# A macaron encoder block: score runs of one half of the heads over four banks, and the last output tile in two halves

## The chip, the cores and the metric

One core of a Trainium2 chip runs the whole block: two feed-forward parts, a recurrence (RG-LRU), neighbourhood attention and the projections between them, all in float32. The metric is the device time in microseconds. A profile of one execution shows each engine: PE is TensorE (matmuls), DVE is VectorE, ACT is ScalarE, SP issues most DMAs.

## The reference, cut to what matters

```python
def _neighbourhood_attention(q, k, v, rpb):          # 16 heads of 64, tokens on an 8 x 64 grid
    ...
    def row_block(args):
        ...
        s = jnp.einsum('bnqhd,brnkhd->bnhqrk', q_r, k_r, preferred_element_type=jnp.float32)
        ...
        s = s + jnp.transpose(bias, (0, 2, 3, 1, 4))[None]
        s = jnp.where(mask, s, -jnp.inf)
        shp = s.shape
        p = jax.nn.softmax(s.reshape(shp[:4] + (kr * K_COLS,)), axis=-1).reshape(shp)
        return jnp.einsum('bhnqrk,brnkhd->bnqhd', p.astype(v.dtype), v_r)
...
        y = jax.nn.sigmoid(ga) * y_lru + jax.nn.sigmoid(gb) * y_att
        x = x + y @ w_out[l]

        x = x + FFN_RES * _swiglu(_rmsnorm(x, norm_ffn2[l]), w_ffn2_gu[l], w_ffn2_down[l])
```

The 512 tokens lie on 8 rows of 64. Queries come in four column blocks of 16 columns; each block sees 32 columns of keys in all 8 rows, so a block has 128 queries and 256 keys.

## The kernel before, in words

Activations stand with 128 features on the partitions and 512 tokens along the row. To hold float32 accuracy each operand is cut into a high and a low part, and a product is three matmuls: high by high, high by low, low by high (`mm3`, L144; lines L145 to L147). Weights are loaded by SP, cut by ACT (L118) and DVE (L121), and used in runs of 24 matmuls of 512 columns per output tile.

The instructions are laid out by a planner: it walks them in the order in which the program emits them, and where an instruction's inputs or its buffer aren't ready by the planner's reckoning, it takes a later one that is ready. Each engine's queue then runs in the order so found. The eight PSUM banks are two pools of four: `acc` (the projections' tiles) and `aux` (transposes, scores, attention's output).

Attention is a generator, `heads(hf, ...)` at L710, for each half `hf` of the heads; a feature tile `fi` (four per half) holds two heads, `hp`. The main stream is projections: for the second half it is the gates (`gates`, L842, one tile of 24 matmuls per call). After each tile `weave` (L449) moves the generator on, by 0.75 steps for a gates tile, so that one step, or none, lies behind each tile. `until` (L462) moves it on by force where a result is needed. The steps of a half:

- `start(fi)` (L727): 4 transposes of q and 4 of k into two `aux` banks (L731, L733), and four copies out of them: qh and kh on ACT (L737, L739), ql and kl on DVE (L738, L740).
- `scores(fi, n2)` (L744): column blocks 2 n2 and 2 n2 + 1. For each block the three products (qh, kh), (qh, kl), (ql, kh), each for both heads; a head is 64 of the 128 rows of the array, and the two heads write two different `aux` banks (L757). That is a run of twelve matmuls. Behind it come, per head and block, the read with bias and maximum on DVE (L767), the exponential on ACT (L770), and the scaling by the sum on DVE (L772, L776). The read frees the bank.
- `turn(fi, n2, hp)` (L780): 4 transposes of p into an `aux` bank (L784), copied out by ACT (L786).
- `apply(fi)` (L789): 32 matmuls of p by v, which use 64 columns of the array each (L795), into an `aux` bank, copied out by ACT (L804).

The loop at L809 to L829 sets the order: eight units (fi, n2); a unit's `turn` comes one unit later and `apply` of a tile two units after its second half, right behind that unit's scores (the order is fixed by `after`, L199). `start(fi + 1)` stands behind the first unit of tile fi.

At the end `ffn` (L334) does the down projection in two groups of four output tiles. For the first 16 of the 22 feature tiles the four outputs advance together (`put_in`, L426); then each output does its last 6 feature tiles alone, is scaled on DVE (L442) and handed to `out2` (L899), which adds the residual (L901) and writes 256 KB (L902).

Of the kernel before, what the change touches and what calls it, by code (L numbers as in the profile page):

```python
# [12 lines left out]
ALU = mybir.AluOpType  # L13
# [3 lines left out]
P = 128  # L17
T = 512
D = 1024
KT = D // P  # L20
# [26 lines left out]

DTAIL = 3

AHEAD = 4  # L50
NWARM = 8

# [1 line left out]

LRU_F = 4

ATT_LAG = 1, 2

RATE = {
    "xr": {"lru": 4, "att": 0.0},  # L60
# [7 lines left out]
def block_kernel(ctx: ExitStack, tc, a, out):  # L68
# [18 lines left out]
    def big_t(dt=F32, shape=(P, T), n="b"):  # L87
        return big.tile(list(shape), dt, tag="big", bufs=NBIG, name=nm(n))
# [4 lines left out]
    def acc_t():  # L93
        return acc.tile([P, T], F32, tag="acc", name=nm("acc"))

    def aux_t():
        return aux.tile([P, T], F32, tag="aux", name=nm("aux"))
# [43 lines left out]
            split(raw[:, s], H[:, s], L[:, s], act)  # L141
        return H, L

    def mm3(ps, wh, wl, xh, xl, first, last):  # L144
        nc.tensor.matmul(ps, wh, xh, start=first, stop=False)  # L145
        nc.tensor.matmul(ps, wh, xl, start=False, stop=False)  # L146
        nc.tensor.matmul(ps, wl, xh, start=False, stop=last)  # L147

    def feat_chunk(src, nk, xh, xl, ps, k0, ktot, act=True):
        H, L = load_w(src, nk * P, act)  # L150
# [183 lines left out]
    def ffn(wgu, ws, wd, xh, xl, S, ssum, plain, res, emit_out, lead=None):  # L334
        hs = []
        r = None
        pre = {}
        if lead is not None:


            for i in range(NLEAD):
                pre[i] = acc_t() if i < 3 else aux_t()
            wts = [[None] * 2 for _ in range(NLEAD)]
            for k in range(KT):
                lead[0](k)
                if k in LEAD_W:
                    n = LEAD_W[k]
                    o = (k % 4) * P
                    s = slice(o, o + n * P)
                    for i in range(NLEAD):  # L350
                        if k % 4 == 0:
                            wts[i][k // 4] = big_t(n="wraw"), big_t(F32R, n="wh"), big_t(F32R, n="wl")
                        q = nc.scalar if k == 0 and i % 2 == 0 else nc.sync
                        tc.keep_in_program_order(
                            q.dma_start(wts[i][k // 4][0][:, s], wgu[i][:, k * P : (k + n) * P]))
                if k == 0:
                    for raw, H, L in [wts[i][0] for i in range(NLEAD)]:
                        cast = nc.vector.tensor_copy(H[:, s], raw[:, s])
                    after(lead[1](k), cast)
                    for raw, H, L in [wts[i][0] for i in range(NLEAD)]:  # L360
                        nc.vector.tensor_tensor(L[:, s], raw[:, s], H[:, s].bitcast(F32), ALU.subtract)
                else:
                    lead[1](k)
                    if k in LEAD_W:
                        for raw, H, L in [wts[i][k // 4] for i in range(NLEAD)]:
                            split(raw[:, s], H[:, s], L[:, s])
                s = slice((k % 4) * P, (k % 4 + 1) * P)
                w = [wts[i][k // 4] for i in range(NLEAD)]
                lead[2](k)
                if k == KT - 1:  # L370
                    r = rstd(ssum)[0]
                for i in range(NLEAD):
                    nc.tensor.matmul(pre[i], w[i][1][:, s], xh[k], start=k == 0, stop=False)  # L373
                for i in range(NLEAD):
                    nc.tensor.matmul(pre[i], w[i][1][:, s], xl[k], start=False, stop=False)
                for i in range(NLEAD):
                    nc.tensor.matmul(pre[i], w[i][2][:, s], xh[k], start=False, stop=k == KT - 1)

            lead[3]()

        def chunk(i):
            if i in pre:
# [24 lines left out]
        cuts = {}  # L407

        def ahead(n):
            while len(cuts) < min(n, len(order)):  # L410
                qk = order[len(cuts)]
                cuts[qk] = big_t(F32R, n="hh"), big_t(F32R, n="hl")
                split(hs[qk[1]], *cuts[qk])

        strassen(ws, (FT - plain) // 2, A, r, hs, lambda: ahead(AHEAD))
        for q in range(2):
            outs = range(q * 4, q * 4 + 4)
            for i in range(2):
# [7 lines left out]
            def put_in(i, k):  # L426
                H, L = ws_[k // 2]
                c = slice((k % 2) * T + i * P, (k % 2) * T + (i + 1) * P)
                mm3(ps[i], H[:, c], L[:, c], *cuts[q, k], k == 0, k == FT - 1)

            for j in range(FT // 2):
                ws_.append(load_w(wd[q, j], 1024))
                ahead(q * FT + 2 * j + 2 + AHEAD)
                if j < FT // 2 - DTAIL:
                    for k in (2 * j, 2 * j + 1):
                        for i in range(4):
                            put_in(i, k)
            for i, m in enumerate(outs):
                for k in range(FT - 2 * DTAIL, FT):
                    put_in(i, k)  # L440
                t = big_t(n="dn")
                nc.vector.scalar_tensor_tensor(t, ps[i], -0.5, r, ALU.mult, ALU.mult)  # L442
                emit_out(m, t)


    lanes = {"lru": [], "att": []}
# [263 lines left out]
    def heads(hf, raws, st):  # L710
# [30 lines left out]
            grid = lambda t: t.rearrange("p (r c) -> p r c", r=ROWS)  # L741
            qk[fi] = qh, ql, grid(kh), grid(kl)

        def scores(fi, n2):  # L744

            qh, ql, kh, kl = qk[fi]
            if n2 == 0:
                rss[fi] = tiny.tile([P, 2, NCB], F32, tag="rs", name=nm("rs"))
            rs = rss[fi]
            ps = [aux_t() for _ in range(2)]  # L750
            for i in range(2):
                n = n2 * 2 + i
                keys = lambda t: t[:, :, KSTART[n] : KSTART[n] + 2 * QC].rearrange("p r (h c) -> p h r c", h=2)
                for q_, k_ in ((qh, kh), (qh, kl), (ql, kh)):
                    for hp in (1, 0):
                        o = slice(hp * HD, (hp + 1) * HD)
                        mm = nc.tensor.matmul(ps[hp][:, i * 256 : (i + 1) * 256], q_[o, n * P : (n + 1) * P], keys(k_[o]),  # L757
                                         start=k_ is kh and q_ is qh, stop=q_ is ql)
# [53 lines left out]
        LB, LC = ATT_LAG  # L812
        for i in range(len(units) + LC):
            if i < len(units):
                fi, n2 = units[i]
                last = scores(fi, n2)
                if i >= LC and units[i - LC][1]:
                    apply(units[i - LC][0], last)
                if n2 == 0:
# [81 lines left out]
        nc.vector.tensor_tensor(o, ps, xres[m], ALU.add)  # L901
        nc.sync.dma_start(out[m], o)  # L902

    ffn(a["w2gu"], a["w2s"], a["w2d"], xh, xl, forms.S, ssum, NPLAIN[1], lambda m: xd[m], out2)


def layouts(inp):
# [72 lines left out]
```

## Time and profile before

| | |
|---|---|
| median of 3 runs | 1133.14 us (1133.12 to 1133.49) |
| the profiled execution's own time | 1133.02 us |
| its span, first to last instruction | 1130.9 us |
| TensorE busy | 1124.3 us, 99% of the span |
| VectorE busy | 836.0 us, 74% |
| ScalarE busy | 594.7 us, 53% |
| granted TensorE clock, mean | 0.999 of full speed |

The span leaves out what lies around the first and last instruction. Matmuls are pipelined: a printed duration overlaps the next matmul's, so the cost of one is the distance between two starts. The timeline merges neighbouring instructions of one kind into one line.

### The profile page before, as it was taken

The page shows a single profiled execution, that of the slowest core. Times are in us where ns is not written, and L with a number is a line of the kernel's source. Part 1 is how long each engine was busy: PE and PEld are TensorE (multiplying, and loading weights), DVE is VectorE, ACT ScalarE, POOL GpSimd, SP SyncE. Part 2 cuts the span into 40 slices and gives each one's busy share as a digit, 9 for nine tenths or more (in the row PEclk, how much of TensorE's full clock was granted, in tenths as well). Part 3 has the DMA queues.
Part 4 walks back from the last instruction along what each step waited for, and adds up shares of the span by engine and source line. Part 5 has one row for each costly group of instructions (what it writes and reads, how often), then busy time and mean ns, then how long its engine had stood idle before and what let it go on. Part 6 is the DMA issues. An engine that isn't in the chain of part 4 may idle for free.

```text
span 1130.9 us, 17246 instructions
## 1 busy us (share of the span) xinstructions
PE 1124.3 (99%) x6872; PEld 995.1 (88%) x6872; DVE 836.0 (74%) x1288; ACT 594.7 (53%) x896; POOL 19.3 (2%) x52
## 2 busy tenths in 40 slices
PE   9999999999999999999999999999999999999998
PEld 8899999988888888888788888888999999998886
DVE  7898888884836798797855576859688888894542
ACT  8554544563624595985564254656445445464330
POOL 0000000000000000010110000000000000000000
PEclk9999999999999999999999999999999999999999
DMA  7242333443433342353443332355123233352320
GB/s 263 94 131 79 119 102 102 136 137 94 130 94 111 94 159 84 112 167 103 132 149 104 93 103 88 109 169 184 56 93 116 92 112 113 94 168 93 131 75 38
DMA packets 43553, 130.69 MB, mean 116 GB/s; under 512 B 5968, under 2 KB 8272, under 8 KB 43472
## 3 DMA queue, kind: packets, MB, share of 16 engines
q1 hardware_dynamic: 39600, 119.36, 33.8%
q0 software_dynamic: 3296, 9.97, 2.8%
q8 instruction: 54, 0.88, 0.3%
q10 hardware_dynamic: 576, 0.26, 0.1%
q14 instruction: 27, 0.22, 0.1%
HBM read 121.17 MB, written 8.39 MB: 115 GB/s over the span
## 4 chain that ended last, share of the span: by engine, by line
PE 97%; DVE 1%; ACT 1%; issue 0%; DVEq 0%
PE acc L260 29%; PE acc L145 11%; PE acc L146 11%; PE acc L147 11%; PE aux L260 5%; PE aux L145 4%; PE aux L146 4%; PE aux L147 4%; PE acc L666 4%; PE acc L665 3%; PE acc L667 3%; PE aux L784 1%; PE aux L795 1%; PE aux L757 1%; PE acc L373 1%; PE aux L373 0%
## 5 line engine op out<-in xcount | busy, mean ns | idle before, releaser
L118 ACT ACTIVATE wh<-wraw 128x1024 fp32r<-128x1024 f32 (+3 forms) x242 | 241.3, 999 | 333.9 <-PE acc L260 96.8
L121 DVE TENSOR_TENSOR wl<-wraw,wh 128x1024 fp32r<-128x1024 f32 (+3 forms) x254 | 291.4, 1150 | 138.5 <-ACT wh L118 137.9
L260 PE MATMUL acc<-s,wh 128*128 128x256 f32 x1216 | 220.6, 283 | 0.1
L260 PEld LDWEIGHTS acc<-s,wh 128*128 128x128 f32 x1216 | 189.7, 192 | 0.3 <-ACT p L317 0.3
L260 PE MATMUL acc<-s,wl 128*128 128x256 f32 x608 | 172.1, 283 | 0.0
L145 PE MATMUL acc<-xh,wh 128*128 128x512 f32 x304 | 120.2, 395 | 0.0
L146 PE MATMUL acc<-xl,wh 128*128 128x512 f32 x304 | 119.0, 392 | 0.0
L147 PE MATMUL acc<-xh,wl 128*128 128x512 f32 x304 | 118.8, 391 | 0.0
L260 PEld LDWEIGHTS acc<-s,wl 128*128 128x128 f32 x608 | 116.7, 192 | 0.0
L260 PE MATMUL acc<-xh,wl 128*128 128x256 f32 x304 | 86.0, 283 | 0.0
L260 PE MATMUL acc<-xl,wh 128*128 128x256 f32 x304 | 86.0, 283 | 0.0
L260 PE MATMUL acc<-xh,wh 128*128 128x256 f32 x304 | 86.0, 283 | 0.0
L665 PE MATMUL acc<-wh,xh 128*128 128x512 f32 x192 | 75.2, 392 | 0.0
L666 PE MATMUL acc<-wh,xl 128*128 128x512 f32 x192 | 74.8, 390 | 0.0
L667 PE MATMUL acc<-wl,xh 128*128 128x512 f32 x192 | 74.8, 389 | 0.0
L294 DVE TENSOR_TENSOR wraw<-wraw,pair 128x1024 f32<-128x1024 f32 x57 | 69.5, 1220 | 0.8
L145 PE MATMUL aux<-hh,wh 128*128 128x512 f32 x176 | 68.5, 389 | 0.0
L146 PE MATMUL aux<-hl,wh 128*128 128x512 f32 x176 | 68.5, 389 | 0.0
L147 PE MATMUL aux<-hh,wl 128*128 128x512 f32 x176 | 68.5, 389 | 0.0
L145 PE MATMUL acc<-hh,wh 128*128 128x512 f32 x176 | 68.5, 389 | 0.0
L146 PE MATMUL acc<-hl,wh 128*128 128x512 f32 x176 | 68.5, 389 | 0.0
L147 PE MATMUL acc<-hh,wl 128*128 128x512 f32 x176 | 68.5, 389 | 0.0
(194 smaller groups left out, 2197.5 us busy)
## 6 DMA issues: line engine op xcount, KB each, us to landing
wraw<-wqkv SPq DMA_DIRECT2D x24, 512.0 KB, 3.6
wraw<-wg SPq DMA_DIRECT2D x24, 512.0 KB, 3.6
wraw<-w1d SPq DMA_DIRECT2D x22, 512.0 KB, 3.6
wraw<-w2d SPq DMA_DIRECT2D x22, 512.0 KB, 3.6
pair<-w2s SPq DMA_DIRECT2D x20, 512.0 KB, 3.6
wraw<-w2s SPq DMA_DIRECT2D x20, 512.0 KB, 3.6
wraw<-w1s SPq DMA_DIRECT2D x18, 512.0 KB, 3.6
pair<-w1s SPq DMA_DIRECT2D x18, 512.0 KB, 3.6
```

What stands on the lines that cost most here:

```text
L118: nc.scalar.activation(H, raw, AF.Copy)
L121: nc.vector.tensor_tensor(L, raw, H.bitcast(F32), ALU.subtract)
L145: nc.tensor.matmul(ps, wh, xh, start=first, stop=False)
L146: nc.tensor.matmul(ps, wh, xl, start=False, stop=False)
L147: nc.tensor.matmul(ps, wl, xh, start=False, stop=last)
L260: nc.tensor.matmul(o, w_[:, c], x_, start=first and m + k == 0 and w_ is H and x_ is xh_, stop=m + k == 4 and w_ is L, skip_group_check=True)
L294: nc.vector.tensor_tensor(t, t, o, ALU.add)
L373: nc.tensor.matmul(pre[i], w[i][1][:, s], xh[k], start=k == 0, stop=False)
L665: nc.tensor.matmul(pss[j], xh[kk][:, tj], H[:, s], start=kk == 0, stop=False)
L666: nc.tensor.matmul(pss[j], xl[kk][:, tj], H[:, s], start=False, stop=False)
L667: nc.tensor.matmul(pss[j], xh[kk][:, tj], L[:, s], start=False, stop=kk == KT - 1)
L757: mm = nc.tensor.matmul(ps[hp][:, i * 256 : (i + 1) * 256], q_[o, n * P : (n + 1) * P], keys(k_[o]), start=k_ is kh and q_ is qh, stop=q_ ...
```

## The change

In the first half of the heads nothing changes but the order of the three products: k's low part comes first, (qh, kl), (qh, kh), (ql, kh). In the second half a unit is a whole feature tile: its four column blocks are one run of 24 matmuls, the first two blocks into two `aux` banks, the other two into two `acc` banks. The lag of `turn` is one unit and that of `apply` two units, now in units of a tile. A unit has two steps (a `yield` stands between its two halves of `turn`), so the number of steps stays 14.

The last output tile (m = 7) is done in halves of 256 tokens for its last five feature tiles: the first half goes on in the tile's bank, the second half's share goes into a bank of its own, `p2`, and is added on DVE. Each half is written by a DMA of its own.

```diff
+EHALF = 5
...
-ATT_LAG = 1, 2
+ATT_LAG = (1, 2), (1, 2)
...
             for i, m in enumerate(outs):
+                if end is not None and m == KT - 1:
+                    break
                 for k in range(FT - 2 * DTAIL, FT):
                     put_in(i, k)
...
+        i, x, k0 = 3, xres[KT - 1], FT - EHALF
+        for k in range(FT - 2 * DTAIL, k0):
+            put_in(i, k, k0 - 1)
+        t, o, p2 = big_t(n="dn"), big_t(n="o"), aux_t()[:, :half]
+        t0, t1 = slice(0, half), slice(half, T)
+
+        def scaled(p, tok):
+            nc.vector.scalar_tensor_tensor(t[:, tok], p, -0.5, r[:, tok], ALU.mult, ALU.mult)
+
+        for k in range(k0, FT):
+            put_half(ps[i][:, t0], i, k, t0, False, k == FT - 1)
+        for k in range(k0, FT):
+            put_half(p2, i, k, t1, k == k0, k == FT - 1)
+        scaled(ps[i][:, t1], t1)
+        nc.vector.tensor_tensor(o[:, t1], t[:, t1], x[:, t1], ALU.add)
+        scaled(ps[i][:, t0], t0)
+        nc.vector.tensor_tensor(o[:, t0], t[:, t0], x[:, t0], ALU.add)
+        end(t0, o)
+        scaled(p2, t1)
+        nc.vector.tensor_tensor(o[:, t1], o[:, t1], t[:, t1], ALU.add)
+        end(t1, o)
...
-        def scores(fi, n2):
+        def scores(fi, n2s):
...
-            ps = [aux_t() for _ in range(2)]
-            for i in range(2):
-                n = n2 * 2 + i
+            pss = {n2: [aux_t() if n2 == n2s[0] else acc_t() for _ in range(2)] for n2 in n2s}
+            for n in [n2 * 2 + i for n2 in n2s for i in range(2)]:
+                ps, i = pss[n // 2], n % 2
...
-                for q_, k_ in ((qh, kh), (qh, kl), (ql, kh)):
+                for q_, k_ in ((qh, kl), (qh, kh), (ql, kh)):
...
-            for hp in range(2):
+            for n2, hp in [(n2, hp) for n2 in n2s for hp in range(2)]:
+                ps = pss[n2]
...
-        units = [(fi, n2) for fi in range(4) for n2 in range(2)]
+        units = [(fi, (n2,)) for fi in range(4) for n2 in range(2)] if hf == 0 else [(fi, (0, 1)) for fi in range(4)]
...
             if 0 <= i - LB < len(units):
-                for hp in range(2):
-                    turn(*units[i - LB], hp)
-            if len(units) <= i < len(units) + LC and units[i - LC][1]:
+                for n2 in units[i - LB][1]:
+                    for hp in range(2):
+                        turn(units[i - LB][0], n2, hp)
+                    if hf == 1 and n2 == 0:
+                        yield
+            if len(units) <= i < len(units) + LC and 1 in units[i - LC][1]:
                 apply(units[i - LC][0])
             yield
```

The new `put_half` is `put_in` for half the tokens: one feature tile's three matmuls (`mm3`) of 256 columns into a given part of a bank. The new `end` of `ffn` writes one half of the last tile, `out[KT - 1][:, tok]`.

## Rows read from the trace of the kernel before

**Rows 1.** The page, part 1: busy time, share of the span, instructions of each engine.

```profile
PE 1124.3 (99%) x6872; PEld 995.1 (88%) x6872; DVE 836.0 (74%) x1288; ACT 594.7 (53%) x896; POOL 19.3 (2%) x52
```

**Rows 2.** The page, part 4: engines' shares of the chain that ended last.

```profile
PE 97%; DVE 1%; ACT 1%; issue 0%; DVEq 0%
```

**Rows 3.** Timeline, TensorE, first runs, second half: start us, us, engine, line, out<-in.

```profile
655.62 0.39 PE L147 MATMUL acc<-xh,wl 128*128 128x512 f32 x1
...
655.94 0.38 PE L757 MATMUL aux<-kh,qh 64*128 64x256 f32 x2
...
656.16 0.28 PE L757 MATMUL aux<-kl,qh 64*128 64x256 f32 x2
...
656.28 0.28 PE L757 MATMUL aux<-kh,ql 64*128 64x256 f32 x2
...
657.70 0.48 PE L145 MATMUL acc<-xh,wh 128*128 128x512 f32 x1
...
663.35 0.39 PE L757 MATMUL aux<-kh,qh 64*128 64x256 f32 x2
```

**Rows 4.** Timeline, TensorE: ahead of and behind eight transposes without a run.

```profile
643.84 0.40 PE L147 MATMUL acc<-xh,wl 128*128 128x512 f32 x1
...
644.87 0.48 PE L145 MATMUL acc<-xh,wh 128*128 128x512 f32 x1
```

**Rows 5.** Timeline, TensorE: ahead of and behind a run that a product follows.

```profile
684.53 0.39 PE L147 MATMUL acc<-xh,wl 128*128 128x512 f32 x1
...
685.76 0.66 PE L795 MATMUL aux<-PT,v 128*64 128x128 f32 x8
```

**Rows 6.** Timeline, TensorE: a product without a run ahead of it.

```profile
614.52 0.39 PE L147 MATMUL acc<-xh,wl 128*128 128x512 f32 x1
614.84 0.66 PE L795 MATMUL aux<-PT,v 128*64 128x128 f32 x8
...
616.74 0.50 PE L145 MATMUL acc<-xh,wh 128*128 128x512 f32 x1
```

**Rows 7.** Timeline, TensorE: ahead of p's transposes, twice.

```profile
673.30 0.39 PE L145 MATMUL acc<-xh,wh 128*128 128x512 f32 x1
673.81 0.66 PE L784 MATMUL aux<-ident,p 128*128 128x128 f32 x4
...
696.46 0.40 PE L147 MATMUL acc<-xh,wl 128*128 128x512 f32 x1
697.09 0.66 PE L784 MATMUL aux<-ident,p 128*128 128x128 f32 x4 [0.24 <-DVE nmx L767]
```

**Rows 8.** Timeline, ScalarE: first and last exponential behind the run of 655.94.

```profile
659.52 0.51 ACT L770 ACTIVATE p<-so,nmx 128x256 f32<-128x256 f32 x1
...
661.01 0.49 ACT L770 ACTIVATE p<-so,nmx 128x256 f32<-128x256 f32 x1
```

**Rows 9.** Timeline, VectorE: a read of scores, and the copy of kl.

```profile
658.16 0.42 DVE L767 CUSTOM_DVE_ANT_0 so<-aux,bm 128x256 f32<-128x256 f32 x1
...
663.02 0.74 DVE L740 SCALAR_TENSOR_TENSOR kl<-aux,small,kh 128x512 fp32r<-128x512 f32 x1
```

**Rows 10.** Timeline, all engines: the last matmuls and what follows them.

```profile
1125.89 0.39 PE L146 MATMUL acc<-hl,wh 128*128 128x512 f32 x1
...
1126.12 0.39 PE L147 MATMUL acc<-hh,wl 128*128 128x512 f32 x1
1126.55 0.69 DVE L442 SCALAR_TENSOR_TENSOR dn<-acc,rstd 128x512 f32<-128x512 f32 x1 [2.66 <-PE acc L147]
1127.27 0.69 DVE L901 TENSOR_TENSOR o<-dn,pair 128x512 f32<-128x512 f32 x1
```

**Rows 11.** DMA strip, 1127 to 1131 us: 40 slots, busy share in tenths.

```profile
DMA  0000000000000000005999997100000000000000
```

**Rows 12.** Chain in order of time: start us, us, what; 24 matmuls of 256 columns.

```profile
131.93 2.88 PE aux L260 x24
```

**Rows 13.** Groups by form, VectorE: count, busy us, mean ns; 256 columns.

```profile
L211 DVE SCALAR_TENSOR_TENSOR s<-s,xg 128x256 f32<-128x256 f32 x16 | 6.7, 421 | 0.3
```

More of the change, by code (lines that the diff above doesn't have):

```diff
@@ L142, in load_w, with mm3 @@
         return H, L
[L144 to L147, printed above, removed]
+    def mm3(ps, wh, wl, xh, xl, first, last, skip=False):
+        nc.tensor.matmul(ps, wh, xh, start=first, stop=False, skip_group_check=skip)
+        nc.tensor.matmul(ps, wh, xl, start=False, stop=False, skip_group_check=skip)
+        nc.tensor.matmul(ps, wl, xh, start=False, stop=last, skip_group_check=skip)
     def feat_chunk(src, nk, xh, xl, ps, k0, ktot, act=True):
@@ L332, in strassen, with ffn @@
         last_product(prev)
-    def ffn(wgu, ws, wd, xh, xl, S, ssum, plain, res, emit_out, lead=None):
+    def ffn(wgu, ws, wd, xh, xl, S, ssum, plain, res, emit_out, lead=None, end=None):
         hs = []
@@ L424, in ffn, with put_in, put_half @@
             ws_ = []
-            def put_in(i, k):
+            def put_in(i, k, last=FT - 1):
                 H, L = ws_[k // 2]
                 c = slice((k % 2) * T + i * P, (k % 2) * T + (i + 1) * P)
-                mm3(ps[i], H[:, c], L[:, c], *cuts[q, k], k == 0, k == FT - 1)
+                mm3(ps[i], H[:, c], L[:, c], *cuts[q, k], k == 0, k == last)
+            def put_half(o, i, k, tok, first, last):
+                H, L = ws_[k // 2]
+                c = slice((k % 2) * T + i * P, (k % 2) * T + (i + 1) * P)
+                mm3(o, H[:, c], L[:, c], *(t[:, tok] for t in cuts[q, k]), first, last, True)
             for j in range(FT // 2):
@@ L443, in ffn @@
                 emit_out(m, t)
+        if end is None:
+            return
+        i, x, k0 = 3, xres[KT - 1], FT - EHALF
[17 more added lines that the diff above has]
+        end(t1, o)
     lanes = {"lru": [], "att": []}
@@ L742, in start @@
             qk[fi] = qh, ql, grid(kh), grid(kl)
-        def scores(fi, n2):
+        def scores(fi, n2s):
             qh, ql, kh, kl = qk[fi]
-            if n2 == 0:
+            if 0 in n2s:
                 rss[fi] = tiny.tile([P, 2, NCB], F32, tag="rs", name=nm("rs"))
             rs = rss[fi]
-            ps = [aux_t() for _ in range(2)]
-            for i in range(2):
-                n = n2 * 2 + i
+            pss = {n2: [aux_t() if n2 == n2s[0] else acc_t() for _ in range(2)] for n2 in n2s}
+            for n in [n2 * 2 + i for n2 in n2s for i in range(2)]:
+                ps, i = pss[n // 2], n % 2
                 keys = lambda t: t[:, :, KSTART[n] : KSTART[n] + 2 * QC].rearrange("p r (h c) -> p h r c", h=2)
-                for q_, k_ in ((qh, kh), (qh, kl), (ql, kh)):
+                for q_, k_ in ((qh, kl), (qh, kh), (ql, kh)):
                     for hp in (1, 0):
@@ L757, in scores @@
                         mm = nc.tensor.matmul(ps[hp][:, i * 256 : (i + 1) * 256], q_[o, n * P : (n + 1) * P], keys(k_[o]),
-                                         start=k_ is kh and q_ is qh, stop=q_ is ql)
-            for hp in range(2):
+                                         start=k_ is kl, stop=q_ is ql)
+            for n2, hp in [(n2, hp) for n2 in n2s for hp in range(2)]:
+                ps = pss[n2]
                 bm = bms[hf * 4 + fi, hp]
@@ L806, in apply @@
             att[hf * 4 + fi] = at
-        units = [(fi, n2) for fi in range(4) for n2 in range(2)]
+        units = [(fi, (n2,)) for fi in range(4) for n2 in range(2)] if hf == 0 else [(fi, (0, 1)) for fi in range(4)]
         start(0)
         yield
-        LB, LC = ATT_LAG
+        LB, LC = ATT_LAG[hf]
         for i in range(len(units) + LC):
             if i < len(units):
-                fi, n2 = units[i]
-                last = scores(fi, n2)
-                if i >= LC and units[i - LC][1]:
+                fi, n2s = units[i]
+                last = scores(fi, n2s)
+                if i >= LC and 1 in units[i - LC][1]:
                     apply(units[i - LC][0], last)
-                if n2 == 0:
+                if 0 in n2s:
                     if fi < 3:
@@ L902, in out2 @@
         nc.sync.dma_start(out[m], o)
-    ffn(a["w2gu"], a["w2s"], a["w2d"], xh, xl, forms.S, ssum, NPLAIN[1], lambda m: xd[m], out2)
+    ffn(a["w2gu"], a["w2s"], a["w2d"], xh, xl, forms.S, ssum, NPLAIN[1], lambda m: xd[m], out2,
+        end=lambda tok, o: nc.sync.dma_start(out[KT - 1][:, tok], o[:, tok]))
 def layouts(inp):
```

## The prediction

> **What bounds the kernel now.** I read the busy shares first: TensorE is busy 99% of the span, no other engine more than 74% [rows 1]. The chain that ended last says the same from the other side: 97% of it is TensorE [rows 2]. So a change counts here only by what it takes from, or adds to, TensorE's own stream, and by what lies behind the last matmul. Two places are touched: the score runs of the second half of the heads (from 655.9 us on), and the last output tile. I then read TensorE's timeline there by start times, because matmuls are pipelined: the distance from one start to the next is the cost, not the printed duration. A 512-column matmul costs 0.23 us (1125.89 to 1126.12) [rows 10].
>
> **Part 1: fewer score runs.** A run of before is twelve matmuls on 64 of the 128 rows, issued as six pairs that run side by side; within a run a pair costs 0.12 us (656.16 to 656.28) [rows 3], so six cost 0.72. What a whole run costs I take from two stretches that differ by the run alone. With a run ahead of the eight q and k transposes, the last gates matmul starts at 655.62 and the next gates matmul at 657.70: 2.08 us [rows 3]. With the same eight transposes and no run it is 643.84 to 644.87: 1.03 us [rows 4]. The run costs 1.05, so 0.33 us of it is entering and leaving. It can be seen where: 0.32 instead of 0.23 ahead of the first pair, 0.22 instead of 0.12 between the first pair and the second, the rest behind the last pair. A run with the values' product (L795, which uses 64 of the columns) right behind it goes from 684.53 to 685.76, 1.23 us [rows 5]; that product alone is entered in 0.32 (614.52 to 614.84) [rows 6], so this run costs 0.91, of which 0.19 is overhead: the entry to the product is paid with or without it.
> The second half has eight runs: five lead back to full-array work (0.33 each) and three lead into a product (0.19 each), 2.22 us. After the change four runs of twelve pairs are left. By the loop, the first two are followed by transposes and the last two by a product: 2 x 0.33 + 2 x 0.19 = 1.04. All 96 matmuls stay. The third product loses its run ahead of it, but its own entry was in neither sum. So **part 1 takes off 1.18 us**. Bounds: 0.8 if four runs save only the smaller overhead (4 x 0.19), 1.3 if each saves the larger.
> Overhead at both ends of a run is what the rows show. The Trainium skill (TensorEngine Tiling (Array Packing), Key Properties) has a rule for it: changing the tiling mode drains TensorE. By the Trainium skill's other page on it (TensorE: Matmul & The Clock Gate, Step-by-step: what each phase is for) a drain is some 128 cycles, an estimated 0.05 us at 2.4 GHz; eight switches fewer would then give 0.4 us in place of 1.18, and a time of 1132.0. The rows show three times that, so this price gets no chance of its own.
>
> **Part 2: k's low part first.** The same three products in another order: no instruction more, no byte more. What moves is a wait: a run can't start before kl (L740, the last of the four copies of a feature tile) exists, where it used to start on kh and qh. In the first half of the heads, and for tiles 2 and 3 of the second half, two steps of the weave lie between the copies and the run, each with a gates tile of 24 matmuls at least, so I cost it at nothing there. For tile 1 of the second half the cover is gone: its run moves one step forward, to where the run of 663.35 stands now [rows 3], with 24 gates matmuls between the transposes and it. Today ScalarE does four exponentials there (one per 0.50 us: 659.52 to 661.01 is three steps) [rows 8], then the q and k copies, and VectorE ends kl at 663.02 + 0.74 = 663.76 [rows 9]. With eight exponentials in front of the copies kl comes 4 x 0.50 = 2.0 us later, at 665.75. TensorE gets there at 663.35 + 0.72 = 664.07. The gap is 1.7 us. It costs all of that if TensorE's queue holds the run next, and nothing if the planner has put seven matmuls of the next gates tile ahead (7 x 0.23 = 1.6). Queued behind it are that tile's matmuls, so the whole stream waits.
> The trace shows how well such filling works: in front of p's transposes the planner puts in gates matmuls, and what is left over is 673.30 to 673.81, less 0.23, 0.28 us, and 696.46 to 697.09, less 0.23, 0.40 us [rows 7]. These waits are for the score reads (L767) to free banks. I take 0.40 for kl (bounds 0 and 1.7).
>
> **Part 3: banks.** A run now fills four banks, two of them from the pool of the gates. The reads of the first two can begin 0.72 us before the run ends, which helps the transposes that want those banks. The two gates banks are held until the seventh and eighth read. Of four banks, one holds the tile just done, two the run, one is free; the next tile takes that one for 24 x 0.23 = 5.5 us, and eight reads of 0.42 us [rows 9], 3.4 us, are over by then: no wait. The two waits of [rows 7], 0.68 us, become one behind run 1 and one behind run 2, where a product of 1.9 us (614.84 to 616.74) [rows 6] now lies between and covers most: I take 0.28 in all. With the 0.40 for kl, **the waits come out as they went in: 0**, with bounds of -0.7 (both vanish) and +1.7 (the kl gap uncovered).
>
> **Part 4: the last tile by halves.** Before: the last matmul starts at 1126.12, the scaling at 1126.55, the addition at 1127.27, each 0.69 us [rows 10]; then the DMA. TensorE's side: the last five of the 22 feature tiles go from 15 matmuls of 512 columns (15 x 0.23 = 3.45) to 30 of 256. Those cost 0.12 each (24 in 2.88 us) [rows 12], 3.60: plus 0.15. The first half's two DVE steps and the early part of the second (four operations, 1.7 us) lie beside the second half's 15 matmuls (1.8 us). Behind the last matmul one scaling and one addition of 256 columns remain, 0.42 us each [rows 13] in place of 0.69: minus 0.54. The output DMA moved its 256 KB in 0.75 us (the strip has a slot of 0.1 us) [rows 11]; 128 KB at that rate is 0.37: minus 0.37, bounds 0 (rows half as long cost as much) and 0.37. The extra DMA's issue falls a microsecond before the last one. **Part 4 takes off 0.76 us**, bounds 0.4 and 0.8.
>
> **Sum.** -1.18 + 0 - 0.76 = -1.94 us. The profiled execution took 1133.02 us (span 1130.9, 2.1 around it), 0.12 under the median of 1133.14. Set against the median: **1131.2 us**. A difference of 0.2%, 2.3 us, is about what can be told from no change: under 1130.9 or over 1135.4.
>
> **Rivals.**
> *Waits vanish.* The banks of the first half of a run are read earlier, the planner covers kl, and the two waits go: another -0.7 to -1.1, so 1130.2 to 1130.6. For it: a product lies ahead of the transposes in two of the four runs. Against: the 0.28 and 0.40 are left over although gates matmuls fill in [rows 7], and the reads come no faster than now.
> *The reads become the bound; slower.* One run now hands VectorE eight reads and ScalarE eight exponentials at once. The wait that would grow is kl's (1.7), and behind it the transposes of three runs that want banks, each by the four reads more that may stand ahead, 4 x 0.42 = 1.7 us: at most 1.7 + 3 x 1.7 = 6.8, in place of the 0.7 there now. At half of it, 3.4 - 0.7 = +2.7, less 1.9, it gives +0.8: 1133.9. It decides from waits of 2.6 us (0.7 + 1.9) in this half on. Against: the gates matmuls fill, and two of the three have a product as cover. The Trainium skill names this mechanism (TensorEngine Tiling (Array Packing), PSUM Bottleneck: tiling speeds up TensorE but not the emptying of PSUM); in the trace it shows only as the 0.28 and 0.40.
> *It doesn't do what it says.* The second pair of banks isn't free where the run is planned, gates matmuls slip in between, and the eight runs stay: only part 4 is left, 1132.4. For it: the gates' own tile is still to be read. Against: one bank of four is held by it.
>
> **How the numbers follow.** Forecast (1130.9 to 1132.0): 0.55, as it needs only start distances that repeat in all eight runs. Waits vanish: 0.20. Split runs, or a tail that gains nothing: 0.15. Reads become the bound: 0.10, of which 0.03 above 1135.4. Faster than 1130.9: 0.20 and the lower edge of the forecast, 0.23. Slower than 1135.4: 0.03. The same: 0.74. The range runs from 1130.1 (part 1 and 4 at their upper bounds and no waits) to 1133.2 (the kl gap whole and the lower bounds of the rest, and the split runs).
>
> **What would show it.** In the changed profile: four runs of 24 score matmuls in the second half, each 0.12 per pair after the first; 0.32 ahead of a run's first pair; how long TensorE stands ahead of the run of tile 1 near 664 us, and whether kl released it; gates matmuls inside a run (split). At the end: 30 matmuls of 256 columns 0.12 apart, two operations of 0.42 us behind the last of them, and the last DMA's strip half as wide. The forecast is wrong if transposes wait more than a microsecond for L767, if kl's wait is more than 1.7 us, or if other stages, whose code is unchanged, are laid out differently by the planner.

## The result, and the profile after

| | before | after |
|---|---|---|
| median of 8 runs each | 1133.3 us (1133.04 to 1133.73) | 1136.71 us (1135.71 to 1137.25) |
| ratio after / before, 95% interval | | 1.0029 (1.0019 to 1.0038) |
| the profiled execution's own time | 1133.02 us | 1137.16 us |
| its span | 1130.9 us | 1135.4 us |

The change costs 3.4 us where I had forecast a gain of 1.94: slower, beyond the upper end of the range and on the other side of zero. The runs of after fall into two groups, 1135.71 to 1136.33 and 1137.09 to 1137.25, with a mean granted TensorE clock of 0.998 and 0.997; the profiled execution is of the upper one, so its account comes out larger (4.5 us of span) than the medians do.

Part 1 of the page of after (busy us, share, instructions of each engine), beside [rows 1]:

```profile
PE 1125.2 (99%) x6887; PEld 998.0 (88%) x6887; DVE 836.2 (74%) x1292; ACT 594.0 (52%) x896; POOL 19.3 (2%) x52
```

It says almost nothing: TensorE is still busy 99%. What went wrong covers a dozen microseconds of 1135. The waits of TensorE in after (what waited, for whom, us in total, times, longest) are plainer:

```profile
PE aux L791 <- DVE kl L774: 3.7, 1, 3.7
...
PE aux L819 <- ACT att L839: 1.0, 1, 1.0
```

Both are new and lie in the second half of the heads; of the three lines left out two have their like in before, and the third is 0.2 us. L791 is the score matmul (L757 of before), L774 the copy of kl (L740), L819 p's transposes (L784), L839 the copy of attention's output out of its bank (L804).

TensorE's timeline in after around the first of them (start us, us, engine, line, out<-in, and in brackets the idle time and who ended it):

```profile
663.95 0.39 PE L149 MATMUL acc<-xh,wl 128*128 128x512 f32 x1
667.99 0.58 PE L791 MATMUL aux<-kl,qh 64*128 64x256 f32 x2 [3.65 <-DVE kl L774]
668.34 0.45 PE L791 MATMUL aux<-kh,qh 64*128 64x256 f32 x2
668.55 0.45 PE L791 MATMUL aux<-kh,ql 64*128 64x256 f32 x2
...
670.85 1.11 PE L765 MATMUL aux<-ident,qk 128*128 128x128 f32 x4
671.75 1.06 PE L767 MATMUL aux<-ident,qk 128*128 128x128 f32 x4
672.61 1.57 PE L819 MATMUL aux<-ident,p 128*128 128x128 f32 x8
673.94 0.48 PE L147 MATMUL acc<-xh,wh 128*128 128x512 f32 x1
...
696.72 0.40 PE L149 MATMUL acc<-xh,wl 128*128 128x512 f32 x1
698.16 0.66 PE L819 MATMUL aux<-ident,p 128*128 128x128 f32 x4 [1.05 <-ACT att L839]
```

Two things are to be seen. TensorE stands still from 664 to 668. And what comes after that is slow: a pair costs 0.21 us (668.34 to 668.55) where it cost 0.12 in [rows 3], four transposes 0.90 (670.85 to 671.75). The busy time of each engine by stretch in after (stretch, us, then PE, PEld, DVE, ACT, POOL busy with counts, granted TensorE clock, DMA share, GB/s) shows why:

```profile
656.00:664.00 8.00, 8.00 (x57) 6.76 (x56) 7.99 (x30) 6.63 (x18) 0.60 (x2) 1.00 0.30 82
664.00:668.00 4.00, 0.35 (x4) 0.04 (x2) 3.85 (x8) 1.92 (x4) 0.48 (x1) 0.86 0.50 166
668.00:674.00 6.00, 6.00 (x41) 5.78 (x41) 4.32 (x25) 3.86 (x15) 0.54 (x1) 0.53 0.41 112
674.00:680.00 6.00, 6.00 (x31) 5.00 (x30) 2.93 (x8) 2.30 (x6) 0.54 (x1) 1.00 0.35 109
```

The granted clock is 1.00 when TensorE stops, 0.53 over the six microseconds after it starts again (nearly all of it at the lower of the two levels, 1.2 GHz), and 1.00 afterwards. "Busy 6.00" in that stretch is work at half speed; that is why the share of busy time hides it.

By slices of half a microsecond the clock is down before TensorE starts again; this is the first slice that is wholly at the lower level:

```profile
667.00:667.50 0.50, 0.00 (x0) 0.00 (x0) 0.50 (x2) 0.00 (x0) 0.00 (x0) 0.50 0.03 12
```

**The account.** From the first transposes of the second half to the first matmul with w_out: 644.08 to 737.71 in before, 93.63 us; 644.26 to 742.92 in after, 98.66. The difference is +5.03:

| term | us |
|---|---|
| wait for kl: 663.95 to 667.99, 4.04, less the usual entry 0.32 [rows 3] | +3.72 |
| low clock: the run of 24 matmuls 2.86 (the three others 1.65), q and k transposes 1.76 (0.85), p's transposes 1.33 (0.85) | +2.60 |
| wait for the copy of attention's output: 696.72 to 698.16, 1.44, less 0.23 | +1.21 |
| four runs instead of eight (part 1) | -1.18 |
| waits of before that are gone: 0.28 and 0.40 [rows 7]; between 727 and 738 us eight of p's transposes at 1.21 and 0.96 (0.85 and 0.88 are usual there) and a product at 2.10 (1.90 [rows 6]) | -1.32 |
| sum | +5.03 |

The part 1 term is not measured by itself: it is the forecast's own figure, and the sum closes with it. Ahead of this stage after is 0.18 later; behind it, from w_out's first matmul to the end of the span, it is 0.71 faster (393.19 to 392.48), which is part 4. 0.18 + 5.03 - 0.71 = 4.50, the difference of the spans.

**Why kl came so late.** VectorE's timeline in after:

```profile
664.07 0.75 DVE L772 SCALAR_TENSOR_TENSOR ql<-aux,gq,qh 128x512 fp32r<-128x512 f32 x1
...
664.81 0.68 DVE L887 TENSOR_TENSOR pair<-acc,rstd 128x512 f32<-128x512 f32 x1
665.39 0.61 DVE L811 TENSOR_SCALAR p<-p,rs 128x256 f32<-128x256 f32 x2
665.96 1.23 DVE L123 TENSOR_TENSOR wl<-wraw,wh 128x1024 fp32r<-128x1024 f32 x1
667.10 0.74 DVE L774 SCALAR_TENSOR_TENSOR kl<-aux,small,kh 128x512 fp32r<-128x512 f32 x1
```

And the copy of kh, from ScalarE's timeline in after:

```profile
664.31 0.67 ACT L773 ACTIVATE kh<-aux,small 128x512 fp32r<-128x512 f32 x1
```

kh, which kl needs, is there at 664.98, in time for the start that the forecast had for kl (its end at 665.75 less 0.74 is 665.01). But VectorE's queue runs in the order laid out by the planner, and ahead of kl it holds a gates product, two scalings of p and the cut of a weight piece: kl starts 2.1 us after it could and ends at 667.84. In before kh ends at 662.74, and kl starts 0.28 us later, at 663.02 [rows 9]. kh's copy, from ScalarE's timeline in before:

```profile
662.07 0.67 ACT L739 ACTIVATE kh<-aux,small 128x512 fp32r<-128x512 f32 x1
```

### The profile page after: what moved, and what is told of

Same layout as the page of the kernel before. It is cut to its first block, busy times and chain, and to the rows that moved or that the text cites. A ratio compares the mean times of both kernels' runs of the same rounds, so it can differ in the third digit from the quotient of the medians.

```text
span 1135.4 us, 17282 instructions
## 1 busy us (share of the span) xinstructions
PE 1125.2 (99%) x6887; PEld 998.0 (88%) x6887; DVE 836.2 (74%) x1292; ACT 594.0 (52%) x896; POOL 19.3 (2%) x52
## 4 chain that ended last, share of the span: by engine, by line
PE 96%; DVE 2%; ACT 1%; DMA 1%; issue 0%; DVEq 0%
PE acc L262 29%; PE acc L147 11%; PE acc L148 11%; PE acc L149 11%; PE aux L262 5%; PE aux L147 4%; PE aux L149 4%; PE aux L148 4%; PE acc L700 4%; PE acc L699 3%; PE acc L701 3%; PE aux L819 1%; PE aux L830 1%; PE aux L791 1%; DVE so L802 1%; PE acc L377 0%
## 5 line engine op out<-in xcount | busy, mean ns | idle before, releaser
L147 PE MATMUL aux<-hh,wh 128*128 128x512 f32 (+1 forms) x181 | 69.9, 386 | 0.0
L148 PE MATMUL aux<-hl,wh 128*128 128x512 f32 (+1 forms) x181 | 69.9, 386 | 0.0
L149 PE MATMUL aux<-hh,wl 128*128 128x512 f32 (+1 forms) x181 | 69.9, 386 | 0.0
L148 PE MATMUL acc<-hl,wh 128*128 128x512 f32 (+1 forms) x176 | 67.9, 386 | 0.0
L149 PE MATMUL acc<-hh,wl 128*128 128x512 f32 (+1 forms) x176 | 67.9, 386 | 0.0
L147 PE MATMUL acc<-hh,wh 128*128 128x512 f32 (+1 forms) x176 | 67.9, 386 | 0.0
```

Source lines behind the costliest of these rows:

```text
L147: nc.tensor.matmul(ps, wh, xh, start=first, stop=False, skip_group_check=skip)
L148: nc.tensor.matmul(ps, wh, xl, start=False, stop=False, skip_group_check=skip)
L149: nc.tensor.matmul(ps, wl, xh, start=False, stop=last, skip_group_check=skip)
```

## The experiments

Each kernel was timed beside the kernel before on the same chip. The theories, as I had them when I began: **A**: the loss is the wait for kl and the low clock that follows it, and both go when kl is in time. **B**: the loss is the burst, eight reads and eight exponentials at once behind each run; with kl in time transposes wait for reads and copies instead.

| kernel | us, median | ratio to before, 95% |
|---|---|---|
| e1_tail: only the end | 1132.58 | 0.9995 (0.9986 to 1.0005) |
| e16_loworder: only kl first | 1133.28 | 1.0 (0.999 to 1.0009) |
| e2_heads: all but the end | 1137.21 | 1.0035 (1.0022 to 1.0048) |
| e4_filler: TensorE kept busy in the wait | 1134.51 | 1.0012 (1.0003 to 1.0021) |
| e6_klprio: kl's copy earlier | 1133.81 | 1.0003 (0.9994 to 1.0013) |
| e5_khfirst: old order of products | 1132.33 | 0.9991 (0.9982 to 1.0) |
| e10_claimacc: the run's gates banks claimed early | 1132.19 | 0.999 (0.9981 to 1.0) |
| e3_early: tile 1's q and k one step earlier | 1132.42 | 0.9993 (0.9984 to 1.0002) |
| e11_late: e3 and p's transposes one step later | 1129.99 | 0.9971 (0.9959 to 0.9983) |
| e17_latekh: e11 with the old order | 1130.06 | 0.997 (0.9958 to 0.9983) |

The kernel before took 1133.25 to 1133.30 each time, so the lines can be compared with each other. Where an interval takes in 1, a change against the kernel before is not shown by the times alone. Against the changed kernel all but e2_heads stand clear: their highest single time (1134.92, e4_filler) lies under its lowest (1135.71).

### Which part of the change

**e1_tail.** The kernel before with the last output by halves; against the changed kernel:

```diff
-        units = [(fi, (n2,)) for fi in range(4) for n2 in range(2)] if hf == 0 else [(fi, (0, 1)) for fi in range(4)]
+        units = [(fi, (n2,)) for fi in range(4) for n2 in range(2)]
...
-                for q_, k_ in ((qh, kl), (qh, kh), (ql, kh)):
+                for q_, k_ in ((qh, kh), (qh, kl), (ql, kh)):
...
```

> The kernel before with the last output tile by halves alone; the heads as before, products in the old order. If the tail's sum is right (one scaling and one addition of 256 columns in place of 512, half the last DMA, 0.15 us more of matmuls), it is 0.7 us faster than before: 1132.6. If the shorter DMA brings nothing: 1132.9. If the halves cost what they bring: 1133.3.

Measured: 1132.58, 0.67 under the kernel before (1133.25), where part 4 had 0.76. The interval takes in 1; the steps behind the last matmul show the gain more plainly. The tail of e1_tail, all engines:

```profile
1126.97 0.42 DVE L464 SCALAR_TENSOR_TENSOR dn<-aux,rstd 128x256 f32<-128x256 f32 x1 [0.37 <-PE aux L149]
1127.43 0.42 DVE L476 TENSOR_TENSOR o<-o,dn 128x256 f32<-128x256 f32 x1
```

Two operations of 0.42 us behind the last matmul, where [rows 10] has two of 0.69. The output DMA's strip in after (1131.4 to 1135.4 us, slots of 0.1 us) has two transfers of some four slots, in place of the one of seven and a half of [rows 11]:

```profile
DMA  0000000000799700000000299940000000000000
```

**e16_loworder.** The kernel before with the new order of the products alone, in both halves of the heads:

```diff
-                for q_, k_ in ((qh, kh), (qh, kl), (ql, kh)):
+                for q_, k_ in ((qh, kl), (qh, kh), (ql, kh)):
...
```

> The kernel before with k's low part first, and nothing else of the change: eight runs in two banks of the transposes' pool, the last tile in one piece. If the new order costs only where a run also claims banks of the gates' pool (theory A2), it changes nothing here: 1133.0 to 1133.5. If holding a run back for kl costs anywhere, it is slower by some of the 0.3 to 0.7 us that such waits take: 1133.7 or more.

Measured: 1133.28 beside 1133.26. With eight short runs the order costs nothing: two steps of the weave lie between the copies and the run.

**e2_heads.** The changed kernel with the last output in one piece:

```diff
-    ffn(a["w2gu"], a["w2s"], a["w2d"], xh, xl, forms.S, ssum, NPLAIN[1], lambda m: xd[m], out2,
-        end=lambda tok, o: nc.sync.dma_start(out[KT - 1][:, tok], o[:, tok]))
+    ffn(a["w2gu"], a["w2s"], a["w2d"], xh, xl, forms.S, ssum, NPLAIN[1], lambda m: xd[m], out2)
```

> The changed kernel with the last output tile as before, in one piece. If the two parts add up, it is 0.7 us slower than the changed kernel: 1137.4, 4.1 over before.

Measured: 1137.21, 0.50 over the changed kernel. The parts add up: the whole loss, some 3.9 us, comes with the long runs, and neither the end nor, with short runs, the order has a share in it.

### The wait and the clock

**e4_filler.** The changed kernel with sixteen matmuls of 512 columns into the run's own first bank ahead of the run of tile 1. Their results are thrown away (the run's first matmul starts the bank anew); they only keep TensorE at work while it waits:

```diff
+            if (hf, fi) == (1, 1):
+                for _ in range(16):
+                    nc.tensor.matmul(pss[0][0], xh[0][:, :P], xh[0], start=True, stop=True)
```

> The changed kernel with 16 matmuls of 512 columns on the full array (3.6 us of work whose result is thrown away) put ahead of the run of tile 1, into the bank that the run overwrites. They need no kl. If the slow run behind the wait is the clock's answer to the idle engine, the wait is filled, the granted clock stays at 1.0, the run takes 1.65 us again in place of 2.86 and the eight transposes 0.85 in place of 1.76: 2.6 us less than the changed kernel, about 1134.1. If the run is slow for its operands or its banks, it stays slow: 1136.7.

TensorE's timeline in e4_filler:

```profile
664.49 3.79 PE L787 MATMUL aux<-xh 128*128 128x512 f32 x16
668.31 0.39 PE L794 MATMUL aux<-kl,qh 64*128 64x256 f32 x2
...
669.96 0.66 PE L765 MATMUL aux<-ident,qk 128*128 128x128 f32 x4
```

Two stretches of e4_filler, columns as above:

```profile
664.00:668.00 4.00, 4.00 (x19) 3.19 (x18) 4.00 (x9) 2.25 (x5) 0.54 (x1) 1.00 0.60 180
668.00:674.00 6.00, 5.97 (x52) 5.20 (x51) 4.79 (x27) 4.19 (x16) 0.82 (x2) 1.00 0.44 126
```

Measured: 1134.51. Nothing useful is done in the wait, and from the last gates matmul to the run it lasts as long as in after, 4.04 us (664.27 to 668.31). But the clock stays at 1.00, the run takes 1.65 us (668.31 to 669.96), and the stage is 2.56 us shorter than in after (96.10 against 98.66); by the medians 2.2, and 2.6 to 2.7 against the executions of after at 0.997, of which the profiled one is. So the 2.60 in the account is the clock's, and the clock fell because TensorE stood still.

**e6_klprio.** The changed kernel with kl's copy ahead of the other work on VectorE:

```diff
-            nc.vector.scalar_tensor_tensor(kl, pk, gk, kh.bitcast(F32), ALU.mult, ALU.subtract)
+            with tc.high_priority():
+                nc.vector.scalar_tensor_tensor(kl, pk, gk, kh.bitcast(F32), ALU.mult, ALU.subtract)
```

> The changed kernel with kl's copy given the planner's high priority; on VectorE it then stands ahead of one pair of scalings (0.61 us) and one split of weights (1.23 us), 1.8 us earlier. TensorE still has no gates matmuls ahead of the run. The wait should fall from 3.7 to 1.9 us. If the clock falls all the same: 1134.9. If the shorter wait leaves the clock up: 1132.3.

Measured: 1133.81, between the two expected times, because both outcomes occur: four of its ten executions have a mean granted clock of 1.000 and take 1132.72 to 1133.15, one has 0.999 (1133.50), and five have 0.998 and take 1134.12 to 1134.43. The profiled one is of the five. kl's copy in VectorE's timeline of e6_klprio:

```profile
665.19 0.75 DVE L775 SCALAR_TENSOR_TENSOR kl<-aux,small,kh 128x512 fp32r<-128x512 f32 x1
```

TensorE's timeline in e6_klprio:

```profile
663.74 0.39 PE L149 MATMUL acc<-xh,wl 128*128 128x512 f32 x1
665.99 0.39 PE L792 MATMUL aux<-kl,qh 64*128 64x256 f32 x2 [1.86 <-DVE kl L775]
666.21 0.28 PE L792 MATMUL aux<-kh,qh 64*128 64x256 f32 x2
666.34 0.28 PE L792 MATMUL aux<-kh,ql 64*128 64x256 f32 x2
...
666.78 0.41 PE L792 MATMUL aux<-kh,ql 64*128 64x256 f32 x2
666.99 0.41 PE L792 MATMUL acc<-kl,qh 64*128 64x256 f32 x2
```

Two stretches of e6_klprio:

```profile
664.00:668.00 4.00, 2.14 (x23) 2.01 (x24) 4.00 (x10) 1.74 (x5) 0.27 (x1) 0.82 0.50 157
668.00:674.00 6.00, 6.00 (x36) 5.24 (x33) 5.74 (x27) 6.00 (x20) 1.07 (x2) 0.83 0.62 197
```

kl starts 1.9 us earlier (665.19 against 667.10) and the wait is 1.93 us in place of 3.72. That is close to the forecast's own bound of 1.7: kh ends at 664.77, and with only the gates product left ahead of kl on VectorE the gap is about what I had reckoned. What I had no term for is there all the same in this execution: the run begins at full speed (0.12 a pair), and in its middle, with TensorE already at work again, the pairs go to 0.21. The run takes 2.41 us and the q and k transposes 1.68: some 1.6 us for the clock. The executions at 1.000 are about 1.3 us shorter: the same wait costs the clock in one execution and little or nothing of it in another.

### Why nothing filled the wait

**e5_khfirst.** The changed kernel with the old order of the products; kl is then needed later in the run.

```diff
-                for q_, k_ in ((qh, kl), (qh, kh), (ql, kh)):
+                for q_, k_ in ((qh, kh), (qh, kl), (ql, kh)):
...
-                                         start=k_ is kl, stop=q_ is ql)
+                                         start=k_ is kh and q_ is qh, stop=q_ is ql)
```

> The changed kernel with the products in the old order, k's high part first. Theory A: the wait is for kl whichever product is first; the run of tile 1 starts one pair earlier and then waits inside, 3 us or more, time within 0.5 us of the changed kernel, 1136.2 to 1137. Rival: it is the new order that costs, since it holds back pairs that kh would allow; then 1133 to 1134.

Measured: 1132.33; the rival was right that the order costs, and the time is lower still than it had. kl comes just as late, at 666.99, and yet the time goes down by 4.4 us. TensorE's timeline in e5_khfirst:

```profile
663.85 0.39 PE L149 MATMUL acc<-xh,wl 128*128 128x512 f32 x1
664.92 0.39 PE L791 MATMUL aux<-kh,qh 64*128 64x256 f32 x2 [0.69 <-ACT kh L773]
665.15 0.28 PE L791 MATMUL acc<-kh,qh 64*128 64x256 f32 x2
...
665.77 0.48 PE L147 MATMUL acc<-xh,wh 128*128 128x512 f32 x1
...
667.95 0.40 PE L147 MATMUL acc<-xh,wh 128*128 128x512 f32 x1
668.27 0.39 PE L791 MATMUL aux<-kl,qh 64*128 64x256 f32 x2
```

The run is split: four matmuls open the banks, two aux and two acc, then transposes and ten gates matmuls (665.77 to 668.27) fill the time until kl, then the other twenty. The order of the products has no part in kl's lateness; kl first takes away the filling. Theory A's cause changed with this to **A2**: the next gates tile gets its bank from the pool `acc` in the program's order, behind the two `acc` banks of the run. With kl first these two are opened only when kl is there, so the gates matmuls can't be put ahead.

**e10_claimacc.** A2 put to the test. The changed kernel, kl first, with two matmuls of 64 columns into the run's two `acc` banks ahead of it; their results are thrown away:

```diff
+            if (hf, fi) == (1, 1):
+                for b in pss[1]:
+                    nc.tensor.matmul(b[:, :64], xh[0][:, :P], xh[0][:, :64], start=True, stop=True)
```

> The changed kernel with two small matmuls (64 columns, result thrown away) into the two gates-pool banks of the run of tile 1, put ahead of that run. They need no kl; they only claim the two banks early. Theory A2 (with k's low part first nothing of the run can be issued before kl, so its two gates-pool banks are claimed late, and the next gates tile, which stands behind them in that pool, can't be put ahead of the run as a filler): gates matmuls stand ahead of the run again, 14 of them by the order of the instructions, the wait shrinks from 3.7 us to under 0.8 and the clock stays up: 1132.2 to 1132.9, as with k's high part first. Rival (the wait is kl's lateness alone, whatever is claimed): 1136 to 1137.

TensorE's timeline in e10_claimacc:

```profile
664.05 0.30 PE L787 MATMUL acc<-xh 128*128 128x64 f32 x2
664.19 0.48 PE L147 MATMUL acc<-xh,wh 128*128 128x512 f32 x1
...
667.23 0.39 PE L148 MATMUL acc<-xl,wh 128*128 128x512 f32 x1
667.86 0.39 PE L794 MATMUL aux<-kl,qh 64*128 64x256 f32 x2 [0.24 <-DVE kl L774]
```

One stretch of e10_claimacc:

```profile
664.00:668.00 4.00, 3.75 (x19) 2.85 (x20) 3.72 (x8) 1.79 (x4) 0.35 (x1) 1.00 0.50 167
```

Measured: 1132.19. Two small matmuls that compute nothing win 4.5 us. Fourteen gates matmuls (664.19 to 667.23) now stand where TensorE had stood still, kl's wait is down to 0.24, and the granted clock is 1.00. e5_khfirst and e10_claimacc both bear A2 out: not kl's lateness by itself, but that lateness together with banks that the run claims late, stopped TensorE. That it is the two `acc` banks, and not any early matmul, follows from the order in which the program asks for banks, and no run shows it apart: e4_filler opens an `aux` bank alone and has no gates matmul ahead of the run (664.49 to 668.31), but its sixteen matmuls take up the wait themselves.

### The burst, and a version without it

**e3_early.** The changed kernel with tile 1's q and k transposed and copied together with tile 0's, so that kl is there long before its run:

```diff
         start(0)
+        if hf == 1:
+            start(1)
         yield
...
-                    if fi < 3:
+                    if fi < 3 and (hf, fi) != (1, 0):
                         start(fi + 1)
```

> The changed kernel, but in the second half of the heads the transposes and copies of tile 1 are emitted with those of tile 0, one step earlier, so that kl of tile 1 is there long before its run. Theory A (the run waits 3.7 us for kl, and the idle engine's clock then falls, 2.6 us more): both go, 6.3 us less than the changed kernel, about 1130.4, and no granted clock under 0.9 between 656 and 700 us. Theory B (a run over four banks hands VectorE and ScalarE too much at once, and some wait follows it wherever the copies stand): a wait of 2 us or more appears at the next transposes, 1133 to 1136.

Measured: 1132.42, 2 us above what A had for it and 0.6 under the least that B had. kl's wait and the low clock are gone (clock 1.00 from 656 to 674 us, the run 1.65). But TensorE in e3_early waits behind the run of tile 1, and for the copy of attention's output as in after:

```profile
666.58 0.60 PE L767 MATMUL aux<-ident,qk 128*128 128x128 f32 x4
668.36 0.66 PE L819 MATMUL aux<-ident,p 128*128 128x128 f32 x4 [1.18 <-DVE nmx L802]
```

1.34 us there and 1.21 behind: 2.55 us of waits in this half, where before had 1.32. B is right for these: p's transposes need a bank that the burst of reads or the burst of exponentials has yet to free.

**e11_late.** e3_early with all sixteen of p's transposes of a tile in the second of its two steps, behind one gates tile more:

```diff
             if 0 <= i - LB < len(units):
+                if hf == 1:
+                    yield
                 for n2 in units[i - LB][1]:
                     for hp in range(2):
                         turn(units[i - LB][0], n2, hp)
-                    if hf == 1 and n2 == 0:
-                        yield
```

> The changed kernel with tile 1's transposes and copies one step early (as in the run before) and with all sixteen transposes of p of a tile in the second step of its unit, a gates tile behind the score run, in place of eight in each step. What waited for the reads (1.34 us) and for attention's copy (1.21 us) then has 24 matmuls ahead of it. If these waits are the rest of what ate the gain: 4 runs in place of 8 (-1.18), the tail (-0.7) and all waits of before gone (-1.3) make 1130.1. If the burst of reads and exponentials costs in some other way, it stays at 1132 or above.

Measured: 1129.99 (1129.68 to 1130.47), 3.3 us under the kernel before and 6.7 under the changed one. It is faster than both kernels. The view of the waits shows none for TensorE in this half any more. TensorE's timeline in e11_late, the run of tile 1 straight behind the gates matmuls, and p's transposes:

```profile
663.73 0.39 PE L149 MATMUL acc<-xh,wl 128*128 128x512 f32 x1
664.05 0.38 PE L791 MATMUL aux<-kl,qh 64*128 64x256 f32 x2
...
672.10 2.19 PE L819 MATMUL aux<-ident,p 128*128 128x128 f32 x16
674.05 0.48 PE L147 MATMUL acc<-xh,wh 128*128 128x512 f32 x1
```

These sixteen transposes take 1.95 us where those of tile 2 take 1.66 (716.93 to 718.59): 0.29 is what is left of the waits. The stage takes 91.44 us (644.00 to 735.44), 2.19 less than before: 1.18 for the runs and the 1.32 of before's waits, less this 0.29, make 2.21.

**e17_latekh.** e11_late with the old order of the products, by the same lines as e5_khfirst:

```diff
-                for q_, k_ in ((qh, kl), (qh, kh), (ql, kh)):
+                for q_, k_ in ((qh, kh), (qh, kl), (ql, kh)):
```

> The fastest kernel so far (tile 1's transposes and copies one step early, sixteen transposes of p in a unit's second step) with k's high part first. With kl there in time the order should make no difference: 1129.7 to 1130.3, as with the low part first (1129.99). If the low part first brings something of its own, this is 0.4 us or more slower.

Measured: 1130.06, the same. With kl in time the order is worth nothing either way; it cost 4.4 us (the changed kernel less e5_khfirst) only where kl was late.

## Why the prediction was wrong, point by point

**Part 1, right.** At full clock a run costs 1.64 to 1.65 us from its first pair to what follows (all four in e11_late), which is twelve steps of 0.12 and 0.2 more, as reckoned. The term was not measured apart, but the accounts of after and of e11_late both close with 1.18, to 0.02 us.

**Part 2, the step that failed.** The mechanism was named: tile 1 of the second half loses its cover and kl's wait stands there. Its size was wrong, 3.72 us where I took 0.40 with an upper bound of 1.7 (more than 1.7 was the forecast's own sign of being wrong), and so was its price, in three places.
- The bound itself. I moved before's kl by the 2.0 us of four exponentials, and with it the 0.28 us that VectorE let pass there after kh's end. kh came 2.24 later, so it is luck that its end, 664.98, falls on my start of kl, 665.01. But VectorE was not as free as in before: a gates product, two scalings and a weight's cut stood in its queue ahead of kl, 2.1 us from kh's end in place of 0.28. e6_klprio moves kl ahead of the scalings and the cut and finds 1.93, close to my 1.7.
- The choice inside the bounds. I took 0.40 from [rows 7], since the planner had filled other gaps with gates matmuls. Those gaps wait for `aux` banks, which the gates don't use. This wait holds two `acc` banks back, and the gates' next tile is behind them (e5_khfirst, e10_claimacc). The row I leaned on was of another kind of wait.
- A term that was missing. I priced an idle TensorE by its idle time alone. What follows it runs at half the clock for a while: 2.60 us behind 3.7 us of idling, some 1.6 behind 1.9 in the profiled execution of e6_klprio, which about half of its executions share. No row of before could show it, as the longest wait of TensorE in before is 1.1 us; the forecast should have said that the price of the kl gap had no upper bound from rows.

**Part 3, half right.** I asked whether a bank of the four was free, and found that none would be waited for. That was the wrong question: what counted was who claims a bank of the pool first. Of the waits behind the runs the 0.68 and more of before did go, as "waits vanish" had it, and one of 1.21 came instead, for a bank that attention's output held while its copy stood behind exponentials on ScalarE (ScalarE's timeline in after):

```profile
697.53 0.57 ACT L839 ACTIVATE att<-aux 128x512 f32<-128x512 f32 x1
```

It stands behind seven exponentials that start 0.49 us apart from 694.08 on; the transposes of 698.16 start as the copy ends. I had counted the burst on VectorE only, and this copy not at all.

**Part 4, right.** -0.71 in the profile and -0.67 in e1_tail (whose interval takes in 1), for -0.76; the two operations behind the last matmul are the 0.42 us each that it had.

**Part 2 elsewhere, right.** In the first half and for tiles 2 and 3 the new order costs nothing (e16_loworder, e17_latekh).

**The rivals.** "The reads become the bound; slower" gave the right sign by half the right mechanism: its first item was kl's wait, capped by the same 1.7, and its chance of ending above 1135.4 was 0.03. The rest of it, waits for banks behind the burst, is real but small: 2.55 us in e3_early where it is alone, of which 1.34 is for the reads that the rival named and 1.21 for attention's copy, which it did not. "It doesn't do what it says" did not happen: the runs were whole in after. I had listed split runs as a loss; where the run does split, in e5_khfirst, it is what saves the time.

**The range.** Its ends do not quite follow from the terms: parts 1 and 4 at their upper bounds with no waits give 1130.4, not 1130.1, and the upper end of 1133.2 comes out if the 1.7 takes the place of the 0.40, so +1.3 and not the +1.7 given for the waits. It decides nothing: 1136.71 is 3.5 above.

**What stays open.** The two groups of after, and those of e6_klprio, differ in their granted clock (0.997 and 0.998; 0.998 and 1.000). Why the same wait costs one execution more of the clock than another is not shown. That the sum of e3_early's waits would be there in after without kl's wait is likely, but after hides it.

## What to carry to other kernels

When an operand that comes last is moved to the front of a run, find its producer in its engine's queue and add up all that stands ahead of it there, not only its inputs. Then ask what else the waiting run holds: if it takes buffers from the pool of the work that ought to fill the wait, that work stands still too, and claiming the buffers early (or starting the run with an operand that is ready) can be worth more than making the late one faster (here 4.5 us against 2.9). A gap on the engine that bounds the kernel is priced with the slow stretch that follows it, and one step more between producer and user costs nothing where the bounding engine has other work.

## What the runs showed of the hardware

TensorE's clock fell in a kernel whose TensorE is 99% busy, behind a single stop. In after it fell to the lower level while TensorE stood still (0.50 from 667.0 on, the work began at 667.99), and was 0.53 over the 6 us from 668 on, with TensorE busy all of it. After 1.86 us of standing still (e6_klprio) the work began at full clock and went on at the lower one 0.6 us later, while TensorE was busy; in four of ten executions of that kernel the mean clock stayed at 1.000. The Trainium skill (TensorE: Matmul & The Clock Gate, What's actually happening) says that the gate follows how busy TensorE has been recently, and that there are two levels, 1.2 and 2.4 GHz. The traces agree: the granted clock goes between 1.00 and 0.50, a pair of score matmuls takes 0.12 us or 0.21, and sixteen matmuls without use keep it at 0.12 (e4_filler).
